# Second MLP product: seven block products over pairs of blocks in a computed order, and modulation sums at other places

## The chip, the cores and the metric

The kernel runs on one core of one Trainium2 chip. Its engines are TensorE (PE in the profile, PEld its weight loads), VectorE (DVE), ScalarE (ACT), GpSimd (POOL) and SyncE (SP, which issues most transfers). The metric is the device time in microseconds (us) of one execution, as the median over runs; lower is better.

## The reference

```python
D_MODEL, SEQ, DEPTH, D_FF = 1024, 1024, 2, 4096
def sqrelu_mlp(h, w1, w2):
    a = jax.nn.relu(h @ w1)
    return (a * a) @ w2
def reference(x, c, w_ada, b_ada, ...):
    cs = jax.nn.silu(c)
    for i in range(DEPTH):
        mod = cs @ w_ada[i] + b_ada[i]                      # modulation
        sh1, sc1, gt1, sh2, sc2, gt2 = jnp.split(mod, 6, axis=-1)
        h = modulate(rmsnorm(x, norm_mix[i]), sh1, sc1)     # h * (1 + scale) + shift
        y = s5_mixer(...) if i % 2 == 0 else gla_mixer(...)
        x = x + gt1[:, None, :] * y
        h = modulate(rmsnorm(x, norm_mlp[i]), sh2, sc2)
        x = x + gt2[:, None, :] * sqrelu_mlp(h, w_ff1[i], w_ff2[i])
    return rmsnorm(x, norm_final)
```

All of it is float32, for one sequence of 1024 tokens. The S5 mixer of layer 0 is a diagonal complex state-space layer followed by `z = gelu(y); val, gate = split(z @ w_glu); val * sigmoid(gate)`, the product called GLU product below. The mixer of layer 1 is gated linear attention (GLA).

## The kernel before

The program runs its stages one after the other: the S5 mixer (0 to about 165 us in the trace), the GLU product (to about 380), the first MLP (to about 1130), GLA (to about 1560), the second MLP (to about 2160) and the last norm. The residual x stays on chip (`big`, 8 tiles of 128 tokens).

**Products.** A float32 operand is split into a high part h (ACT copies and rounds) and a low part l (DVE subtracts, L56 in the profile), and a product is three matmuls in `mm3` (L215, L216, L217): h·h, h·l, l·h. A full matmul here takes a 128x128 weight and a 128x512 moving tile and writes one PSUM bank; there are eight banks, tags `mm` and `tp`.

**The MLP.** D_FF is cut into 16 blocks of 256 columns (NFB = 16). For each block the first product is made as seven products of half-size blocks (`squares`; 7 products x 4 k x 3 = 84 matmuls), for which `load_a` loads two tiles of W1, builds the sums s, r0[1], r1[0] on POOL and splits them. `activate` makes the squared ReLU (ACT Relu, DVE max-and-multiply) and its split; `load_w2` loads W2, multiplies it by the gate gt2 on POOL (128x1024) and splits it. The second product is the ordinary one (`ff2`, in `plain`): 8 token tiles x 2 f x 2 halves x 3 = 96 matmuls, and 16 additions of a 128x512 PSUM bank to `big` on DVE. The main loop is

```python
        A = plain(0, A)
        T4 = sums()
        for b in range(1, NFB - 1):
            A = plain(b, A)
        plain(NFB - 1, A)
```

A framework places the instructions by the order of the code and by the state of each engine; inside `manual_schedule` an engine takes them exactly in the order written. The functions `winograd`, `quadrants`, `square` and `pair` stand in the file, but nothing calls them.

**The S5 mixer** follows a hand-made string of steps, S5ORD, under `manual_schedule`: u, l, e, k, p, s, o are the steps (each with its parts) of eight groups; p builds the rotation tables `rot`, k the kernels `Ks`, `kd` and `Tb` with transfers through memory, s the states, o the output `z`.

**Modulation sums.** Each of ten rows of `mod` is made by `ada_sum` (eight 512 KB tiles of w_ada, one DVE operation on 128x1024 for each, into the single buffer `adacc`, tag `nrow`) and `ada_row` (two PE matmuls at L191 over the partitions, an addition of the bias, and, for the rows that scale a norm, a multiplication by the norm's weight, which is loaded into the same `nrow` buffer). Six of them are placed in the loop of the GLU product, which goes over 4 column blocks j and 8 token tiles t, 24 full matmuls each.

Of the kernel before, what the change touches and what calls it, by code (L numbers as in the profile page):

```python
# [43 lines left out]
def trunk_kernel(ctx, tc, x, c, w_ada, b_ada, norm_mix, norm_mlp, s5_a_re, s5_a_im, s5_log_dt, s5_b_re, s5_b_im,  # L44
# [20 lines left out]
    def act(out, a, f, **kw):  # L65
        S.activation(out=out, in_=a, func=f, **kw)  # L66
# [147 lines left out]
    def mm3(pst, ah, al, bh, bl, first, last, **kw):  # L214
        T.matmul(pst, ah, bh, start=first, stop=False, **kw)  # L215
        T.matmul(pst, ah, bl, start=False, stop=False, **kw)  # L216
        return T.matmul(pst, al, bh, start=False, stop=last, **kw)  # L217
# [584 lines left out]
        for kt in range(KT):  # L802
            mm3(pst, hh[:, kt, :], hl[:, kt, :], w[kt][0][:, cs], w[kt][1][:, cs], kt == 0, kt == KT - 1)

    def winograd(nk, slot, sink, after=None):

        U = [bank() for _ in range(4)]
        V = []
        for i, (chain, start, th, dh, first) in enumerate((
                (U, True, 0, 0, True), (V, True, 0, 0, False), (V, True, 1, 1, True), (U, False, 0, 1, True),
                (V, False, 0, 1, False), (U, False, 1, 1, False), (U, False, 1, 0, True))):
            if i == 1:
                V += [bank(), bank(), bank("tp"), bank("tp")]
            for k in range(nk):
                a, (bh, bl) = slot(i, k)
                ins = after and after(i, k)  # L820
                with tc.issue_after(ins) if ins else nullcontext():
                    for t in range(4):
                        mm3(chain[t], *a(t), bh, bl, start and k == 0, k == nk - 1, skip_group_check=True)
            for t in range(4):
                sink(4 * th + t, dh, chain[t], first)

    def quadrants(A, W, e, tiles):

        A11, A12, A21, A22 = A
        W11, W12, W21, W22 = W  # L830

        def sums(i):
            for n, o, a, b, op in ((2, A21, A21, A22, ALU.add), (2, W12, W12, W11, ALU.subtract),
                                   (3, A21, A21, A11, ALU.subtract), (3, W12, W22, W12, ALU.subtract),
                                   (4, A12, A12, A21, ALU.subtract), (5, A21, A22, A21, ALU.subtract),
                                   (5, W21, W21, W12, ALU.subtract), (5, W12, W12, W11, ALU.subtract)):
                if n == i:
                    for x, y, z in zip(o, a, b):
                        tt(x, y, z, op, e if op == ALU.subtract else V)

        def slot(i, k):
            if k == 0:
                sums(i)
            a, w = ((A11, W11), (A12, W21), (A21, W12), (A21, W12), (A12, W22), (A21, W12), (A22, W21))[i]
            r = []
            for v, c in zip((a[k], w[k]), tiles()):
                h, l = c[:, :512], c[:, 512:1024]
                if len(v.shape) == 3:
                    split(h.rearrange("p (t x) -> p t x", t=4), l.rearrange("p (t x) -> p t x", t=4), v)
                else:  # L850
                    split(h, l, v)
                r.append((h, l))
            (ah, al), b = r
            return lambda t: (ah[:, P * t:P * t + P], al[:, P * t:P * t + P]), b
        return slot
# [85 lines left out]

    NFB = FF // (2 * P)

    def mlp(i, R, xt, lay, keep, turn, finish):

# [119 lines left out]
        def square(c, sq):
            if c is sq:
                stt(sq, c, 0.0, c, ALU.max, ALU.mult)
            else:
                act(sq, c, AF.Relu)
                stt(sq, c, 0.0, sq, ALU.max, ALU.mult)  # L1070

        def plain(b, A):

            last = b == NFB - 1
# [44 lines left out]
                ff2(t)  # L1119
            return A  # L1120

        def pair(b, A):


            W = []
            for k in range(2):
                for dh in range(2):
                    r = rot("w2", [P, 2, 512], 4, F32)
                    ds_ = slice(512 * dh, 512 * dh + 512)
                    nc.sync.dma_start(out=r, in_=w_ff2[i, 256 * (b + k):256 * (b + k) + 256, ds_].rearrange(  # L1130
                        "(k p) d -> p k d", p=P))
                    tt(r, r, gt2[:, ds_].unsqueeze(1).to_broadcast([P, 2, 512]), ALU.mult, G)
                    W.append(r)
            Q = []
            for k in range(2):
                X = [rot("a2", [P, 2, 512], 4, F32) for _ in range(2)]
                squares(A, [((x_[:, 0], x_[:, 1]), lambda f, c, sq: square(c, sq)) for x_ in X])
                Q += X
                if k == 0:
                    A = load_a(b + 1)  # L1140
            Q[1], Q[2] = Q[2], Q[1]

            def sink(t, dh, pst, first):
                y = xt(t)[:, 512 * dh:512 * dh + 512]
                tt(y, pst, y, ALU.add)

            cut = lambda v: [v[:, k] for k in range(2)]
            winograd(2, quadrants([cut(v) for v in Q], [cut(v) for v in W], G,
                                  lambda: [rot("rg", [P, 1024], 7) for _ in range(2)]), sink)
            return load_a(b + 2)  # L1150
# [385 lines left out]
```

## Time and profile before

| what | value |
| --- | --- |
| time, median of 3 runs (lowest, highest) | 2189.99 us (2188.33, 2190.81) |
| profiled execution: time / span | 2189.98 us / 2188.3 us |
| granted TensorE clock, mean | 0.987 |
| PE busy, instructions | 2112.1 us (97%), 10857 |
| DVE busy, instructions | 1447.4 us (66%), 2004 |
| ACT busy, instructions | 692.9 us (32%), 1163 |
| POOL busy, instructions | 397.0 us (18%), 294 |
| HBM traffic | 164.45 MB read, 10.40 MB written |

Times are from the start of the span. "Busy" is the time covered by an engine's instructions; matmuls overlap each other, so 97% for PE says that it seldom stood still, not that each matmul was as fast as it can be. In a group of instructions `big<-mm,big` reads: written tile, then read tiles. A number in brackets behind a row is idle time of that engine ahead of it, and what ended it.

### The profile page before, as it was taken

The page shows a single profiled execution, that of the slowest core. Times are in us where ns is not written, and L with a number is a line of the kernel's source. Part 1 is how long each engine was busy: PE and PEld are TensorE (multiplying, and loading weights), DVE is VectorE, ACT ScalarE, POOL GpSimd, SP SyncE. Part 2 cuts the span into 40 slices and gives each one's busy share as a digit, 9 for nine tenths or more (in the row PEclk, how much of TensorE's full clock was granted, in tenths as well). Part 3 has the DMA queues.
Part 4 walks back from the last instruction along what each step waited for, and adds up shares of the span by engine and source line. Part 5 has one row for each costly group of instructions (what it writes and reads, how often), then busy time and mean ns, then how long its engine had stood idle before and what let it go on. Part 6 is the DMA issues. An engine that isn't in the chain of part 4 may idle for free.

```text
span 2188.3 us, 26758 instructions
## 1 busy us (share of the span) xinstructions
PE 2112.1 (97%) x10857; PEld 1726.8 (79%) x10857; DVE 1447.4 (66%) x2004; ACT 692.9 (32%) x1163; POOL 397.0 (18%) x294
## 2 busy tenths in 40 slices
PE   5988999999999999999899999999999999999998
PEld 4887777788888888888687877787788888888886
DVE  8996767966656656656732366738875665665666
ACT  5772114322222222222511443314322222222223
POOL 0000001222213213222500000001122222222223
PEclk9999999999999999999899999999999999999999
DMA  8234670111111111112343114421111111111112
GB/s 257 57 89 166 228 241 23 39 58 58 49 49 58 49 49 58 49 49 75 132 144 100 49 34 143 150 77 38 41 48 49 58 48 49 58 49 49 58 49 106
DMA packets 107655, 176.58 MB, mean 81 GB/s; under 512 B 10462, under 2 KB 76102, under 8 KB 107468
## 3 DMA queue, kind: packets, MB, share of 16 engines
q1 hardware_dynamic: 97164, 168.71, 24.3%
q10 hardware_dynamic: 10368, 6.16, 1.3%
q8 instruction: 85, 1.39, 0.3%
q14 instruction: 38, 0.31, 0.0%
HBM read 164.45 MB, written 10.40 MB: 80 GB/s over the span
## 4 chain that ended last, share of the span: by engine, by line
PE 88%; DVE 6%; DMA 3%; ACT 2%; issue 1%; POOL 0%; SPq 0%; ACTq 0%; POOLq 0%; DVEq 0%
PE mm L216 27%; PE mm L215 27%; PE mm L217 27%; DMA stg<-in_w_ada_dram 1%; DVE tmp L56 1%; PE tp L609 1%; PE mm L1362 1%; PE tp L210 1%; PE mm L1342 1%; PE mm L704 1%; DMA stg<-in_s_w_glu_dram 0%; PE mm L658 0%; DVE adacc L59 0%; DMA stg<-in_gla_w_out_dram 0%; DVE nk L59 0%
## 5 line engine op out<-in xcount | busy, mean ns | idle before, releaser
L56 DVE TENSOR_TENSOR big<-mm,big 128x512 f32<-128x512 f32 x528 | 343.0, 684 | 91.3 <-PE mm L217 86.3
L216 PE MATMUL mm<-w,a 128*128 128x512 f32 x1024 | 386.7, 392 | 0.5 <-DVE w L56 0.5
L217 PE MATMUL mm<-w,a 128*128 128x512 f32 x1024 | 384.8, 390 | 0.0
L215 PE MATMUL mm<-w,a 128*128 128x512 f32 x1024 | 365.1, 390 | 2.6 <-ACT w L66 2.6
L216 PE MATMUL mm<-l,rg 128*128 128x512 f32 x904 | 356.3, 394 | 4.7 <-DVE l L56 4.7
L217 PE MATMUL mm<-h,rg 128*128 128x512 f32 x904 | 355.0, 393 | 0.5 <-DVE rg L56 0.5
L215 PE MATMUL mm<-h,rg 128*128 128x512 f32 x904 | 351.1, 394 | 2.4 <-ACT h L66 1.8
L56 DVE TENSOR_TENSOR wk<-mm,wk 128x512 f32<-128x512 f32 (+1 forms) x100 | 68.8, 688 | 381.5 <-PE mm L217 312.5
L215 PE MATMUL mm<-wh,hT 128*128 128x512 f32 (+1 forms) x768 | 291.1, 381 | 2.5 <-ACT hT L66 1.7
L56 POOL TENSOR_TENSOR wk<-wk 128x512 f32<-128x512 f32 (+1 forms) x122 | 160.3, 1324 | 732.3 <-DVE wl L56 307.4
L217 PE MATMUL mm<-wh,hT 128*128 128x512 f32 (+1 forms) x768 | 290.3, 378 | 0.0
L216 PE MATMUL mm<-wl,hT 128*128 128x512 f32 (+1 forms) x768 | 289.6, 378 | 0.1
L56 POOL TENSOR_TENSOR wk<-wk,row 128x1024 f32<-128x1024 f32 x64 | 163.1, 2549 | 610.2 <-DMA wk<-in_w_ff_dram 405.4
L216 PEld LDWEIGHTS mm<-w,a 128*128 128x128 f32 x1024 | 192.3, 188 | 46.4 <-DVE w L56 7.3
L215 PEld LDWEIGHTS mm<-w,a 128*128 128x128 f32 x1024 | 191.3, 188 | 44.6 <-ACT w L66 3.5
L217 PEld LDWEIGHTS mm<-w,a 128*128 128x128 f32 x1024 | 192.3, 188 | 39.1
L66 ACT ACTIVATE wk<-mm 128x512 f32<-128x512 f32 x140 | 83.4, 597 | 422.7 <-PE mm L217 419.0
L216 PEld LDWEIGHTS mm<-l,rg 128*128 128x128 f32 x904 | 170.6, 189 | 43.1 <-DVE l L56 5.6
L215 PEld LDWEIGHTS mm<-h,rg 128*128 128x128 f32 x904 | 170.2, 188 | 41.5 <-ACT h L66 2.3
L217 PEld LDWEIGHTS mm<-h,rg 128*128 128x128 f32 x904 | 170.5, 189 | 39.0 <-DVE rg L56 0.8
L66 ACT ACTIVATE rg<-wk 128x1024 fp32r<-128x1024 f32 (+1 forms) x126 | 114.2, 952 | 266.1 <-POOL wk L56 264.7
L215 PEld LDWEIGHTS mm<-wh,hT 128*128 128x128 f32 x768 | 144.7, 189 | 40.1 <-issue 3.9
(244 smaller groups left out, 2615.8 us busy)
## 6 DMA issues: line engine op xcount, KB each, us to landing
wk<-in_w_ff_dram SPq DMA_DIRECT2D x128, 512.0 KB
stg<-in_w_ada_dram SPq DMA_DIRECT2D x80, 512.0 KB
stg<-in_gla_w_in_dram SPq DMA_DIRECT2D x17, 512.0 KB
stg<-in_s_w_glu_dram SPq DMA_DIRECT2D x32, 256.0 KB
row<-mod SPq DMA_DIRECT2D x10, 512.0 KB
wada<-in_w_ada_dram SPq DMA_DIRECT2D x9, 512.0 KB
big<-in_x_dram SPq DMA_DIRECT2D x8, 512.0 KB
Tb<-kd ACTq DMA_DIRECT2D x8, 512.0 KB
```

Source lines behind the costliest of these rows:

```text
L56: (e or V).tensor_tensor(out=out, in0=a, in1=b, op=op)
L66: S.activation(out=out, in_=a, func=f, **kw)
L210: ins = T.transpose(pt[:, P * k:P * k + P], h[:, P * (4 * q + k):P * (4 * q + k + 1)], ident)
L215: T.matmul(pst, ah, bh, start=first, stop=False, **kw)
L216: T.matmul(pst, ah, bl, start=False, stop=False, **kw)
L217: return T.matmul(pst, al, bh, start=False, stop=last, **kw)
L609: T.matmul(pts[i][:, P * q:P * q + P], t[i][k][:, P * q:P * q + P], (nident if i < k else ident), start=q == 0 and k == 0, stop=q == 3 and ...
L704: T.matmul(Yp[r][:, P * q:P * q + P], X[rr, i, q, :], E[rr, i // 2, q, :], start=False, stop=(q == 3 and i == 3))
L1342: T.matmul(kvp[c2][hp2][:, 256 * (h % 2):256 * (h % 2) + 256], kz[t % 2][cr, P * h:P * h + P], vo[cr, t, 256 * h:256 * h + 256], start=Tru ...
L1362: T.matmul(op[h // 2][64 * c2:64 * c2 + 64, 256 * (h % 2):256 * (h % 2) + 256], qT[:, h, n0:n0 + 64], Sc[c2][:, h, :], start=True, stop=True)
```

## The change

1. Blocks 1 to 14 of each MLP run as seven pairs (`pairs`, n = 7). The second product of a pair, (1024 tokens x 512 columns) times (512 x 1024), is made by seven products of blocks A11 to A22 and W11 to W22 and eight sums of them (S*, T*): 7 products x 2 halves x 4 token tiles x 3 = 168 matmuls for two blocks. The results of some products accumulate in the same banks (`U`, `V`), and each bank is added to `big` at up to seven places (28 additions to `big` per pair, 16 per block before).
2. All DVE, ACT and PE steps of the pairs stand in one string, PAIRORD, under `manual_schedule`; the number behind the point says of which pair or block a step is. P0 to P6 are the products of the first product, c/x its copies and additions, r and q Relu and Square on ACT, da loads of W1, a1 to a4 the sums of W1, hr0, hs, hr1, hd and lr0 ... their splits, dW loads of W2, gateW their multiplication by the gate, SnA / TnW the sums for product n, hAsh, hWsh and lAsh, lWsh the splits for product s, half h, Msht three matmuls for token tile t, kst an addition to `big`. Of its 238 steps, the start, the piece of the middle that the prediction speaks of, and the end:

```
P0.0 hr1.0 k43.-1 ls.0 lr1.0 P1.0 c1.0 k61.-1 dWW12.0 k62.-1 k63.-1 P2.0 a4.0 c7.0 ...
M113.0 k12.0 M200.0 hW30.0 k13.0 M201.0 hA31.0 lW21.0 M202.0 T3W121.0 M203.0 lA30.0 M210.0 lW30.0 hW31.0
M211.0 k02.0 M212.0 k03.0 M213.0 S4A120.0 lA31.0 M300.0 hA40.0 lW31.0 M301.0 hW40.0 S4A121.0 M302.0 k20.0
hA41.0 M303.0 lA40.0 M310.0 hW41.0 lW40.0 M311.0 k21.0 M312.0 k22.0 M313.0 k23.0 M400.0 S5A210.0 M401.0
T5W210.0 hA50.0 M402.0 T5W120.0 M403.0 lA41.0 hW50.0 lW41.0 S5A211.0 M410.0 T5W211.0 hA51.0 M411.0 T5W121.0
M412.0 k30.0 hW51.0 M413.0 lA50.0 hA60.0 lW50.0 hW60.0 k31.0 hA61.0 M500.0
... dWW11.1 M610.0 k41.0 hs.2 M611.0 lr0.2 M612.0 k60.0 M613.0 k42.0
```

3. In the pairs nothing is left on POOL: the sums of W1 and the gate multiplications are DVE's (128x512), and the squared ReLU is ACT's alone. Seven buffers `rg` serve all splits.
4. `load_a` splits r0, s, r1 in this order. The unused functions are gone.
5. The modulation sums of the GLU loop stand at other (j, t), and S5ORD is another string, in which the p steps stand earlier.

```diff
@@ the loop of the GLU product
-            if j < 3 and t in (1, 5):
+            if (j, t) in ((0, 4), (1, 0), (1, 4), (2, 0), (2, 2), (2, 5)):
                 acc = ada_sum(*ADA[0])
-            if j < 3 and t in ((4, 7) if j == 2 else (3, 7)):
+            if (j, t) in ((0, 7), (1, 2), (1, 7), (2, 1), (2, 4), (2, 7)):
                 ada_row(*ADA.pop(0), acc)
@@ the S5 mixer (the string's middle, cut)
-    S5ORD = "[ s0 s1 S7 S6 ... e5 l4 p4:v k4 e5 o2 p4 s3 k4 l4 e6 p4 k5 ... p7:v k7 p7 k7 s6 p7 s7 s6 o5 s7 o6 k7 s6 s7 o6 s7 s7 o6 o7 o7 o7 ]"
+    S5ORD = "[ s0 s1 S7 S6 ... p6:v e6 s5 p6 e6 u6 p6 s4 k6 l6 ... p7:v e7 s6 p7 e7 u7 p7 s5 k7 l7 k6 o5 k7 u7 s6 l7 o5 ... o7 o7 o7 ]"
@@ load_a
-            for r in (r0, r1, s):
+            for r in (r0, s, r1):
@@ mlp
-        def pair(b, A):
...
+        def pairs(A, n):
+            PROD = ((0, "U", B11), (1, "G", T3), (5, "U", T2), (2, "H", B21), (4, "U", T1), (3, "G", T4), (6, "U", B22))
+            SLOT = (("A11", "W11"), ("A12", "W21"), ("A21", "W12"), ("A21", "W12"), ("A12", "W22"), ("A21", "W12"),
+                    ("A22", "W21"))
+            SINK = ((0, 0), (0, 0), (1, 1), (0, 1), (0, 1), (1, 1), (1, 0))
+            SUM = {"2A21": ("A21", "A22", ALU.add), "2W12": ("W12", "W11", ALU.subtract),
+                   "3A21": ("A21", "A11", ALU.subtract), "3W12": ("W22", "W12", ALU.subtract),
+                   "4A12": ("A12", "A21", ALU.subtract), "5A21": ("A22", "A21", ALU.subtract),
+                   "5W21": ("W21", "W12", ALU.subtract), "5W12": ("W12", "W11", ALU.subtract)}
...
+            def second(f, p):
+                b = 2 * p + 1
+                if f[:2] == "dW":
+                    t = W.setdefault(p, {})[f[2:]] = rot("w2", [P, 2, 512], 4, F32)
+                    nc.sync.dma_start(out=t, in_=w_ff2[i, ...].rearrange("(k p) d -> p k d", p=P))
+                elif f[0] == "g":
+                    tt(t, t, gt2[:, 512 * dh:512 * dh + 512], ALU.mult)
+                elif f[0] in "ST":
+                    tt(quad(p, f[2:5], h), quad(p, x, h), quad(p, y, h), op_)
+                elif f[0] in "hl":
+                    if f[0] == "h":
+                        c = sp_[f[1:]] = rot("rg", [P, 1024], 7)
+                        act(c[:, :512], src, AF.Copy)
+                    else:
+                        tt(c[:, 512:], src, f32(c[:, :512]), ALU.subtract)
+                elif f[0] == "M":
+                    if f == "M000":
+                        UV["V"], UV["U"] = [bank(), bank()], []
+                    if f == "M100":
+                        UV["V"] += [bank("tp"), bank("tp")]
+                    mm3(UV["UVVUVUU"[s]][t], a[...], a[...], w[:, :512], w[:, 512:],
+                        s < 3 and h == 0, h == 1, skip_group_check=True)
+                else:
+                    tt(y, UV["UVVUVUU"[s]][t], y, ALU.add)
...
         A = plain(0, A)
         T4 = sums()
-        for b in range(1, NFB - 1):
-            A = plain(b, A)
-        plain(NFB - 1, A)
+        plain(NFB - 1, pairs(A, NFB // 2 - 1))
```

**VectorE in the MLP.** First what stands there in a block before, from the second product's first additions to `big` to the next block's activations (`a` and `w` are splits of the activations and of W2, `rg` of W1, `wk` unsplit tiles).

```order
L56 TENSOR_TENSOR big<-mm,big 128x512 x2
L56 TENSOR_TENSOR a_5231<-wk,a_5231 128x512
L56 TENSOR_TENSOR big<-mm,big 128x512 x7
L56 TENSOR_TENSOR rg<-wk,rg 128x1024 x2
L56 TENSOR_TENSOR big<-mm,big 128x512
L56 TENSOR_TENSOR rg<-wk,rg 128x1024
L56 TENSOR_TENSOR big<-mm,big 128x512 x2
L56 TENSOR_TENSOR rg<-wk,rg 128x512
L56 TENSOR_TENSOR big<-mm,big 128x512 x4
L56 TENSOR_TENSOR wk<-mm,wk 128x512
L59 SCALAR_TENSOR_TENSOR wk<-wk 128x512
```

In the changed kernel, the stretch of a pair from the additions k22, k23 to the split lW50, in the first MLP (`a_...` and `w_...` are now the unsplit activations and gated W2, `rg` every split).

```order
L56 TENSOR_TENSOR big<-tp,big 128x512 x2
L56 TENSOR_TENSOR a_5310<-a_5454,a_5310 128x512
L56 TENSOR_TENSOR w_5312<-w_5312,w_5293 128x512
L56 TENSOR_TENSOR w_5293<-w_5293,w_5236 128x512
L56 TENSOR_TENSOR rg<-a_5436,rg 128x512
L56 TENSOR_TENSOR rg<-w_5319,rg 128x512
L56 TENSOR_TENSOR a_5310<-a_5454,a_5310 128x512
L56 TENSOR_TENSOR w_5312<-w_5312,w_5293 128x512
L56 TENSOR_TENSOR w_5293<-w_5293,w_5236 128x512
L56 TENSOR_TENSOR big<-mm,big 128x512
L56 TENSOR_TENSOR rg<-a_5310,rg 128x512
L56 TENSOR_TENSOR rg<-w_5293,rg 128x512
```

Before, the additions to `big` stood in a long run with the four W1 splits strewn in; now they stand one or two at a time between operand sums and the splits that the next matmuls read.

**VectorE in the GLU product.** Before, from just behind the last operation of the fourth sum in the loop to the first of the fifth (`sg` is the gate path, `wl` a split of w_glu).

```order
L56 TENSOR_TENSOR wl<-stg,wh 128x1024 x3
L56 TENSOR_TENSOR sg<-mm,sg 128x256
L56 TENSOR_TENSOR sg<-sg,row 128x256
L56 TENSOR_TENSOR big<-big,sg 128x256
L56 TENSOR_TENSOR wl<-stg,wh 128x1024
L56 TENSOR_TENSOR sg<-mm,sg 128x256
L56 TENSOR_TENSOR wk<-mm,wk 64x512
L56 TENSOR_TENSOR sg<-sg,row 128x256
L56 TENSOR_TENSOR big<-big,sg 128x256
L59 SCALAR_TENSOR_TENSOR wk<-wk,nrow 64x512
L63 TENSOR_SCALAR adacc<-stg,csil 128x1024
```

After, from the same sum's last operations (its row scales a norm) to the first of the fifth.

```order
L56 TENSOR_TENSOR sg<-mm,sg 128x256
L56 TENSOR_TENSOR sg<-sg,row 128x256
L59 SCALAR_TENSOR_TENSOR adacc<-stg,csil,adacc 128x1024
L56 TENSOR_TENSOR big<-big,sg 128x256
L59 SCALAR_TENSOR_TENSOR adacc<-stg,csil,adacc 128x1024 x2
L56 TENSOR_TENSOR sg<-mm,sg 128x256
L59 SCALAR_TENSOR_TENSOR adacc<-stg,csil,adacc 128x1024
L56 TENSOR_TENSOR sg<-sg,row 128x256
L56 TENSOR_TENSOR big<-big,sg 128x256
L56 TENSOR_TENSOR wk<-mm,wk 64x512
L59 SCALAR_TENSOR_TENSOR wk<-wk,nrow 64x512
L63 TENSOR_SCALAR adacc<-stg,csil 128x1024
```

The last operations of the sum stand directly ahead of the row's bias addition `wk<-mm,wk`, and the next sum's first operation (TENSOR_SCALAR) directly behind the row's multiplication.

**ScalarE at the end of S5.** Before, `wh` is a split of w_glu, `LBT`, `Tb` and `kd` belong to the tables, `rot` to the rotation of the last group.

```order
L66 ACTIVATE LBT<-tp 128x512 x2
L640 DMA kd<-Ks 4x32x240 x2
L66 ACTIVATE rot<-tmp 128x512 x2
L66 ACTIVATE wh<-stg 128x1024 x2
L66 ACTIVATE rot<-rot,k_pi_87 128x512
L66 ACTIVATE wh<-stg 128x1024
L711 ACT_TABLE_LOAD
L711 ACTIVATE z<-mm 128x4x8x16 x2
L644 DMA Tb<-kd 128x8x128
```

After:

```order
L66 ACTIVATE rot<-tmp 128x512 x2
L66 ACTIVATE rot<-rot,k_pi_87 128x512
L644 DMA Tb<-kd 128x8x128
L66 ACTIVATE Ks<-tp 128x128 x2
L66 ACTIVATE U<-mm,s_1014 128x128 x8
L711 ACT_TABLE_LOAD
L711 ACTIVATE z<-mm 128x4x8x16 x2
L640 DMA kd<-Ks 4x32x240 x2
L66 ACTIVATE LBT<-tp 128x512
L66 ACTIVATE wh<-stg 128x1024
L66 ACTIVATE LBT<-tp 128x512
L644 DMA Tb<-kd 128x8x128
```

The last group's rotation (`rot`) now stands ahead of the transfers `kd<-Ks` and of the first `wh`, with a group's states and output (`U`, `z`) between.

More of the change, by code (lines that the diff above doesn't have):

```diff
@@ L737, in glu_weights @@
         return wg
-    S5ORD = "[ s0 s1 S7 S6 I0 S2 S3 e0 I0 S5 H1:v S0 S4 S1 e0 T0 H0:v T0 g0 l0 u0:am p0:v e0 e1 g0 g0 e0 u0 g0 u1:am e1 g0 l0 g1 g0 e1 u0 p0 k0 e1 e2 k0 p1:v g1 l0 p0 k0 e2 p1 e2 k0 p1 g2 l1 e2 l0 l1 g2 g1 e3 g2 s0 g1 g2 g1 g3 s0 g1 k0 g2 u1 g2 g3 e3 k1 u2:am e3 s0 k1 u1 l1 k1 s0 k1 p2:v s2 o0 s0 l1 g3 s1 g3 l2 g3 o0 s1 g3 k1 l2 k2 o0 e3 u2 p2 s1 k2 p2 l2 k2 s1 e4 k2 u2 o1 s1 l2 l3 o1 u3:am e4 l3 k2 s3 p3:v k3 e4 o1 s2 p3 e4 u3 e5 k3 p3 l3 s2 u3 k3 s2 l4 k3 l3 s2 u4:am k4 s3 e5 k4 s2 o2 s4 u4 l4 k3 o2 u5:am s3 u4 e5 l4 p4:v k4 e5 o2 p4 s3 k4 l4 e6 p4 k5 s3 s4 l5 o3 k5 s5 s3 u5 k4 u6:am e6 o3 l5 u5 s4 l5 o3 e6 p5:v k5 e6 k5 p5 l5 s4 p5 k6 e7 s5 s4 u6 k6 u7:am o4 l6 s4 k5 s6 u6 e7 o4 l6 s5 l6 o4 e7 p6:v k6 p6 k6 l6 e7 s5 p6 k7 s6 l7 s5 u7 k7 u7 o5 l7 s5 l7 k6 s7 s6 o5 l7 p7:v k7 p7 k7 s6 p7 s7 s6 o5 s7 o6 k7 s6 s7 o6 s7 s7 o6 o7 o7 o7 ]"
+    S5ORD = "[ s0 s1 S7 S6 I0 S2 S3 e0 I0 S5 H1:v S0 S4 S1 e0 T0 H0:v T0 g0 l0 u0:am p0:v e0 p0 g0 g0 e0 u0 p0 g0 l0 g0 e1 g1 g0 u1:am p1:v e1 k0 p1 k0 g1 l0 u0 k0 e1 e2 e1 e2 k0 p1 g2 l1 l0 e2 l1 g2 g1 g2 s0 g1 g2 e2 g1 g2 s0 u1 g1 k0 g2 k1 u2:am g3 p2:v s0 k1 g3 l1 u1 k1 s0 p2 k1 s2 o0 l1 s0 p2 g3 s1 g3 l2 g3 o0 g3 s1 k1 l2 k2 o0 s1 u2 e3 k2 u2 s1 l2 k2 e3 k2 u3:am o1 p3:v e3 p3 l2 e3 p3 s1 k3 s2 l3 k2 k3 o1 s3 s2 l3 u3 o1 k3 s2 l3 e4 k3 u3 s2 l3 e4 o2 u4:am p4:v e4 s3 p4 k3 e4 p4 u4 s2 k4 l4 k4 o2 s4 s3 u4 l4 o2 k4 s3 l4 e5 k4 u5:am s3 l4 e5 o3 s5 p5:v e5 s4 p5 k4 e5 u5 p5 s3 k5 l5 k5 o3 u5 s4 u6:am l5 k5 s4 l5 o3 e6 s4 k5 l5 e6 o4 s6 p6:v e6 s5 p6 e6 u6 p6 s4 k6 l6 k5 o4 k6 u6 s5 u7:am l6 k6 s5 l6 o4 e7 s5 k6 l6 e7 o5 s7 p7:v e7 s6 p7 e7 u7 p7 s5 k7 l7 k6 o5 k7 u7 s6 l7 o5 k7 s6 l7 k7 s6 o6 l7 s6 s7 o6 s7 k7 s7 o6 s7 s7 o7 o7 o7 ]"
     kinds = {"u": feed, "l": tab_lb, "e": tab_e, "k": tab_k, "p": rotation, "s": states, "o": output, "g": group, "I": inputs}
@@ L803, in tok_mm @@
             mm3(pst, hh[:, kt, :], hl[:, kt, :], w[kt][0][:, cs], w[kt][1][:, cs], kt == 0, kt == KT - 1)
[L805 to L855, printed above, removed]
     xs1 = dp.tile([L, D], F32, name="xs1")
@@ L942, in trunk_kernel @@
     NFB = FF // (2 * P)
+    PAIRORD = "P0.0 hr1.0 k43.-1 ls.0 lr1.0 P1.0 c1.0 k61.-1 dWW12.0 k62.-1 k63.-1 P2.0 a4.0 c7.0 dWW21.0 gateW110.0 hd.0 gateW111.0 ld.0 dWW22.0 gateW120.0 da0.1 da1.1 P3.0 c6.0 gateW121.0 gateW210.0 gateW211.0 gateW220.0 P4.0 x1.0 gateW221.0 r1.0 T2W120.0 q1.0 T2W121.0 P5.0 x7.0 r7.0 q7.0 a1.1 a3.1 P6.0 a2.1 hr0.1 x6.0 hs.1 lr0.1 r6.0 ls.1 P0.1 q6.0 r8.0 q8.0 hr1.1 P1.1 lr1.1 c1.1 a4.1 hd.1 P2.1 ld.1 c7.1 hA00.0 da0.2 da1.2 hW00.0 lA00.0 lW00.0 P3.1 c6.1 P4.1 x1.1 r1.1 q1.1 a1.2 P5.1 hA01.0 x7.1 hW01.0 lA01.0 r7.1 lW01.0 q7.1 a3.2 P6.1 hA10.0 x6.1 hW10.0 lA10.0 r6.1 lW10.0 q6.1 S2A211.0 M000.0 a2.2 r8.1 M001.0 q8.1 M002.0 hA11.0 S2A210.0 M003.0 lA11.0 M010.0 hW11.0 M011.0 hA20.0 k00.0 M012.0 lW11.0 M013.0 lA20.0 M100.0 S3A210.0 hW20.0 M101.0 k01.0 hA21.0 M102.0 lW20.0 T3W120.0 M103.0 lA21.0 M110.0 hW21.0 S3A211.0 M111.0 hA30.0 k10.0 M112.0 k11.0 M113.0 k12.0 M200.0 hW30.0 k13.0 M201.0 hA31.0 lW21.0 M202.0 T3W121.0 M203.0 lA30.0 M210.0 lW30.0 hW31.0 M211.0 k02.0 M212.0 k03.0 M213.0 S4A120.0 lA31.0 M300.0 hA40.0 lW31.0 M301.0 hW40.0 S4A121.0 M302.0 k20.0 hA41.0 M303.0 lA40.0 M310.0 hW41.0 lW40.0 M311.0 k21.0 M312.0 k22.0 M313.0 k23.0 M400.0 S5A210.0 M401.0 T5W210.0 hA50.0 M402.0 T5W120.0 M403.0 lA41.0 hW50.0 lW41.0 S5A211.0 M410.0 T5W211.0 hA51.0 M411.0 T5W121.0 M412.0 k30.0 hW51.0 M413.0 lA50.0 hA60.0 lW50.0 hW60.0 k31.0 hA61.0 M500.0 k32.0 M501.0 k33.0 M502.0 lA51.0 M503.0 lW51.0 hW61.0 lA60.0 M510.0 lW60.0 M511.0 k50.0 M512.0 k51.0 M513.0 k52.0 M600.0 hr0.2 k53.0 M601.0 lA61.0 M602.0 lW61.0 M603.0 k40.0 dWW11.1 M610.0 k41.0 hs.2 M611.0 lr0.2 M612.0 k60.0 M613.0 k42.0"
     def mlp(i, R, xt, lay, keep, turn, finish):
@@ L981, in load_a @@
                 parts += [(h[:, :, k], l[:, :, k]) for k in range(2)]
+            parts = parts[:2] + parts[4:] + parts[2:4]
             if b > 0:
@@ L1063, in squares @@
             done[1](0, U, q)
[L1065 to L1070, printed above, removed]
         def plain(b, A):
@@ L1120, in plain @@
             return A
-        def pair(b, A):
[L1125 to L1150, printed above, removed]
```

96 lines of the change are left out of this document (added).

## The prediction

> **What bounds the kernel now.** I read the head of the page first, then the table of engines, the slices, the chain that ended last, two windows of the MLP, and then the timeline where a term needed a duration.
>
> ```profile
> span 2188.3 us, 26758 instructions
> PE 2112.1 (97%) x10857; PEld 1726.8 (79%) x10857; DVE 1447.4 (66%) x2004; ACT 692.9 (32%) x1163; POOL 397.0 (18%) x294
> PE   5988999999999999999899999999999999999998
> PE 88%; DVE 6%; DMA 3%; ACT 2%; issue 1%; POOL 0%; SPq 0%; ACTq 0%; POOLq 0%; DVEq 0%
> ```
>
> TensorE is busy in every slice but the first few (S5), and 88% of the last chain is its own. The two windows are one MLP block each, from one start of POOL's gate product to the next (columns: length, then busy time and count of PE, PEld, DVE, ACT, POOL, then clock, DMA share, GB/s).
>
> ```profile
> 599.07:640.23 41.16, 41.16 (x181) 33.64 (x180) 26.57 (x33) 10.41 (x14) 10.21 (x7) 1.00 0.16 51
> 640.23:681.03 40.80, 40.80 (x180) 33.52 (x179) 25.78 (x33) 10.52 (x14) 10.33 (x6) 1.00 0.17 52
> ```
>
> A block takes 40.80 us for 84 + 96 = 180 matmuls with PE busy throughout: 0.2267 us each. DVE, ACT and POOL have slack. So matmuls taken out pay in full, unless something new makes PE wait.
>
> **Matmuls removed.** A pair had 2 x 96 in its second products and gets 168: 24 fewer, 24 x 0.2267 = 5.44 us. Seven pairs in two MLPs are 14: **-76.2 us**. A pair took 2 x 40.80 = 81.6 us; at PE's pace the new one takes 336 x 0.2267 = 76.2.
>
> **What VectorE gets.** Its load per pair after, by the order: 96 operations on 128x512 (28 additions to `big`, 28 splits, 16 operand sums, 8 gate products, 8 sums of W1, 6 x-additions, 2 splits ld) and 6 splits on 128x1024. The gate, a and the S/T sums are new to it. Their price:
>
> ```profile
> 608.29 0.69 DVE L56 TENSOR_TENSOR wk<-mm,wk 128x512 f32<-128x512 f32 x1 [10.46 <-PE mm L217]
> 609.01 0.69 DVE L59 SCALAR_TENSOR_TENSOR wk<-wk 128x512 f32<-128x512 f32 x1
> 609.62 1.22 DVE L56 TENSOR_TENSOR w<-wk,w 128x1024 fp32r<-128x1024 f32 x1
> 610.76 0.68 DVE L56 TENSOR_TENSOR a<-wk,a 128x512 fp32r<-128x512 f32 x1
> 611.36 0.68 DVE L56 TENSOR_TENSOR wk<-mm,wk 128x512 f32<-128x512 f32 x1
> 614.97 2.89 DVE L59 SCALAR_TENSOR_TENSOR wk<-wk 128x512 f32<-128x512 f32 x1
> 623.35 2.48 DVE L56 TENSOR_TENSOR big<-mm,big 128x512 f32<-128x512 f32 x4
> L56 DVE TENSOR_TENSOR big<-mm,big 128x512 f32<-128x512 f32 x528 | 343.0, 684 | 91.3 <-PE mm L217 86.3
> ```
>
> Four operations one behind the other take 2.48 us, so (2.48 - 0.69)/3 = 0.60 from start to start; 610.76 to 611.36 is 0.60 too, and this one reads no PSUM. An operation that reads what the one ahead wrote starts 0.72 after it (608.29 to 609.01). A 128x1024 split costs 610.76 - 609.62 = 1.14. So 96 x 0.60 + 6 x 1.14 = 64.4 us of the pair's 76.2, where two blocks now take 26.57 + 25.78 = 52.3. It fits as a mean, but not evenly: during the seven products M of the second product (56 x 3 matmuls, 38.1 us) DVE has 61 x 0.60 + 1.14 = 37.7 us. That is where a wait can come, because each half product needs two new splits.
>
> The Trainium skill, VectorE: DVE Perf Modes, section The DRAIN you can't avoid, says that the next operation does not start until the pipeline is empty, and adds that one that is not held starts earlier. By the first sentence an operation would cost its whole 684 ns, and rival B's gentler case (about 2184 us) would be the forecast; the row at 623.35, with 0.60, disagrees.
>
> **The wait in a pair.** I walked the order of DVE and PE through the M part. DVE runs level with PE at k12 and k13, which need the last matmuls of M112 and M113. How soon an addition starts behind its matmul:
>
> ```profile
> 627.06 0.39 PE L217 MATMUL mm<-w,a 128*128 128x512 f32 x1
> 627.48 0.69 DVE L56 TENSOR_TENSOR big<-mm,big 128x512 f32<-128x512 f32 x1 [0.67 <-PE mm L217]
> ```
>
> It starts 0.42 us after the last matmul's start, 0.2 us after PE could issue the next. From k13 to the end of lW50 stand 28 operations (k13, lW21, T3W121, lA30, ... k30, lA50, lW50, the last twelve shown in the order above); three of them read what the one ahead wrote: 28 x 0.60 + 3 x 0.12 + 0.2 = 17.4 us. PE has 24 steps of three matmuls in that time, 24 x 0.68 = 16.3. So M500 waits about 1.0 us for lW50. Five operations later lW51 comes at 20.4 against 20.1: another 0.3. Behind it M600 and M610 find their splits. **+1.3 us per pair, +18 for 14.** What queues behind a late DVE is k31 to k53 and lr0, ls of the next block, with time until P0. From both sides: 0, if DVE is 5% faster than my walk; 4 us per pair, if each of these operations takes the 0.684 of the group's row.
>
> **What is moved off POOL and to ACT.**
>
> ```profile
> L56 POOL TENSOR_TENSOR wk<-wk,row 128x1024 f32<-128x1024 f32 x64 | 163.1, 2549 | 610.2 <-DMA wk<-in_w_ff_dram 405.4 <-DVE wk L56 171.8 <-DVE a L56 20.0
> L56 POOL TENSOR_TENSOR wk<-wk 128x512 f32<-128x512 f32 x120 | 155.5, 1306 | 358.9 <-DVE rg L56 112.5 <-DVE big L56 109.4 <-DMA wk<-in_w_ff_dram 94.6
> L66 ACT ACTIVATE a<-wk 128x512 fp32r<-128x512 f32 x124 | 78.4, 632 | 240.5 <-DVE wk L59 240.4
> ```
>
> POOL waits for others for most of the span, so removing its 10.3 us a block gains nothing by itself; it does away with DVE operations of 2.89 us such as the one at 614.97. ACT gets per pair 28 operand splits, 8 Relu, 8 Square, 6 copies and 2 W1 splits of 128x512 (52 x 0.63) and 6 splits of twice the size (at most 6 x 1.26): about 40 us of 76, no bound. Loads of W1 have to land in time:
>
> ```profile
> 595.27 0.34 SPq L991 DMA_DIRECT2D wk<-in_w_ff_dram  x1
> 599.07 2.40 POOL L56 TENSOR_TENSOR wk<-wk,row 128x1024 f32<-128x1024 f32 x1 [6.71 <-DMA wk<-in_w_ff_dram]
> ```
>
> From issue to use is 3.8 us. In the new order a1 follows da1 by 7 us or more of other work, so I cost it at 0; the cover is P0 to P5 of the block ahead. The W2 loads (four of 512 KB) are issued in P1 to P3 and used by gateW behind them; first uses in the first pair are the tightest. Edges of the pairs: 0 to +2 us per MLP, taken as 0. The order r0, s, r1 and the removed functions: 0, since these splits have slack.
>
> **The GLU stage.** `adacc` is one buffer, so a sum can't start before the row ahead (L191) has read it, and L191 holds PE until its own sum is done.
>
> ```profile
> 206.26 0.62 PE L191 MATMUL mm<-adacc,ones 128*32 128x512 f32 x2
> 225.35 1.28 DVE L59 SCALAR_TENSOR_TENSOR adacc<-stg,csil,adacc 128x1024 f32<-128x1024 f32 x1
> 278.56 0.62 PE L191 MATMUL mm<-adacc,ones 128*32 128x512 f32 x2
> 281.85 0.67 DVE L56 TENSOR_TENSOR wk<-mm,wk 64x512 f32<-64x512 f32 x1
> 302.96 1.28 DVE L59 SCALAR_TENSOR_TENSOR adacc<-stg,csil,adacc 128x1024 f32<-128x1024 f32 x1
> 307.43 0.62 PE L191 MATMUL mm<-adacc,ones 128*32 128x512 f32 x2
> 308.53 0.68 DVE L56 TENSOR_TENSOR wk<-mm,wk 64x512 f32<-64x512 f32 x1 [0.15 <-PE mm L191]
> 322.80 1.28 DVE L59 SCALAR_TENSOR_TENSOR adacc<-stg,csil,adacc 128x1024 f32<-128x1024 f32 x1 [0.76 <-DMA stg<-in_w_ada_dram]
> 325.21 0.62 PE L191 MATMUL mm<-adacc,ones 128*32 128x512 f32 x2
> ```
>
> PE work between rows: five tiles 307.43 - 278.56 = 28.9 us, three tiles 325.21 - 307.43 = 17.8, so 5.55 a tile and, for two, 12.2. A sum needs, from the row ahead to its last end: the second 226.63 - 206.26 = 20.4; the sixth 324.08 - 307.43 = 16.7; the fifth, behind a row with a norm weight to load, 304.24 - 278.56 = 25.7, less 2.2 that its bias addition stood behind a gate operation (3.3 us after the row at 281.85, 1.1 at 308.53) = 23.5. The new positions leave three tiles to the second, two to the fourth, three to the fifth and the sixth: 20.4 - 17.8 = 2.6, 16.7 - 12.2 = 4.5, 23.5 - 17.8 = 5.7, together 12.8 us. A stopped PE also starts slowly:
>
> ```profile
> 178.59 1.09 PE L789 MATMUL tp<-ident,z 128*128 128x128 f32 x4 [4.12 <-DVE hT L56]
> 181.18 0.63 PE L215 MATMUL mm<-wh,hT 128*128 128x512 f32 x1
> 181.60 0.63 PE L216 MATMUL mm<-wl,hT 128*128 128x512 f32 x1
> ```
>
> After 4.12 us of idling the spacing is 0.42 instead of 0.23; some eight matmuls at 0.2 more are 1.6 us, counted once. **+14 us**; bounds 4 (only the fourth waits) and 20 (the slow start after each wait). The Trainium skill, TensorE: Matmul & The Clock Gate, section HAM oscillation, puts such a slow start behind idle gaps over about 3.4 us; the row agrees with it, and by it the fourth's and fifth's waits would each pay the 1.6, which gives 1.6 us more.
>
> **The end of S5.**
>
> ```profile
> 153.53 1.06 ACT L66 ACTIVATE wh<-stg 128x1024 fp32r<-128x1024 f32 x1 [3.73 <-DMA kd<-Ks]
> 155.23 0.69 DVE L56 TENSOR_TENSOR tmp<-mm,rot 128x512 f32<-128x512 f32 x1 [4.25 <-ACT rot L66]
> ```
>
> ACT's queue stood 3.73 us at `wh`, with the last `rot` behind it, and DVE waited 4.25 for that. After, `rot` comes before. **-4 us**; if the transfers, now later in the queue, are late instead, it comes to +4, and if ends further on also close up, -8.
>
> **Sum**, on the profiled execution's 2190.0 (the median of the runs is the same): 2190.0 - 76.2 + 18.2 + 14 - 4 = **2142 us**.
>
> **Rivals.**
> A. The pairs and the loop wait for nothing: then 2190 - 76 - 4 = 2110. For it: the walk's wait is 1.0 of 17 us. Against: the row-to-row distances at the GLU product are short by several us.
> B, the slower side. DVE becomes the bound of the M part, its operations held apart because nearly every one waits for another engine's result, as at 608.29, with 0.72. From S2A210, 1.5 us behind P6's end, to k60 stand 58 operations and a 1024 split: 58 x 0.72 + 1.26 + 1.5 = 44.5 against PE's 38.1, 6.4 over, more than the 5.44 saved: +1 a pair, 2190 + 14 + 14 - 4 = 2214. At 0.684 it is 4.3 over, and 2184. It decides for slower from about 0.69 to 0.70. Against it: 0.60 at 610.76 and 623.35.
> C. Seven `rg` buffers: a split must wait until the half product three ahead has been read, and ACT, DVE and PE then go round in a ring; 0.2 to 0.4 us for each of 14 half products takes away 2.8 to 5.6 a pair: 2165 to 2200. No row of before shows this ring.
> That the pairs don't do what they say is out: by the order PE has 336 rows fewer.
>
> **Chances.** The forecast 0.74, A 0.10, B 0.08, C 0.08. The range is 2110 to 2180: A, the forecast with its own bounds (pairs 0 to 2.5 us of waits each, GLU 4 to 20), and half of C; outside are B and the rest, about 0.2. A measurement of this kernel can tell 0.2% (4.4 us) from no change. Faster: forecast, A, and most of C and some of B, 0.90; same 0.02; slower 0.08, most of B and the end of C.
>
> **What would show it.** Right: PE's count down by 336, a pair from P0 to P0 of about 77.5 us, DVE's window busy share near 0.85, a PE gap of about 1 us ahead of the matmuls M500 that ends with a DVE split, gaps of 3 to 6 us at L191 that end with `adacc`, and no 4 us idle of DVE at the last `rot`. Wrong: DVE start to start above 0.65 in the M part (B), gaps of PE at every half product that end with ACT's splits (C), or W1 sums that wait for a transfer.

## The result and the profile after

The changed kernel takes 2151.24 us (median of 4 runs, 2148.29 to 2153.37) against 2189.26 for the kernel before: ratio 0.9825, 95% interval 0.9808 to 0.9842, 38 us faster. The profiled execution took 2150.91 us with a span of 2149.2. Head of the page, the engines, the chain, and three rows of TensorE's waits (total in us, number of times, longest):

```profile
span 2149.2 us, 26968 instructions
PE 2055.1 (96%) x10521; PEld 1664.6 (77%) x10521; DVE 1624.4 (76%) x2508; ACT 915.9 (43%) x1583; POOL 110.1 (5%) x126
PE 57%; DVE 19%; DMA 2%; POOL 1%; ACT 1%; issue 1%; POOLq 0%; DVEq 0%; ACTq 0%
```

```profile
PE mm L191 <- DVE adacc L59: 10.7, 3, 4.1
PE mm L216 <- DVE rg L56: 8.9, 14, 0.6
PE mm L696 <- DMA Tb<-kd: 4.0, 2, 3.5
```

TensorE has 10857 - 10521 = 336 instructions fewer, as counted. DVE's share of the last chain has gone from 6% to 19%, and three kinds of wait are new: three times at L191 (modulation rows), once in each of the 14 pairs, and twice for `Tb` in S5. Where the 39.1 us of span went, from the first matmul of each stage in both timelines:

| stage (from, to) | before | after | difference |
| --- | --- | --- | --- |
| S5 (0, first GLU matmul) | 173.25 | 176.36 | +3.1 |
| GLU product (to the first MLP's first product) | 203.52 | 219.21 | +15.7 |
| MLP 1 (to GLA's first product) | 682.20 | 653.53 | -28.7 |
| GLA (to the second MLP's first product) | 449.16 | 450.64 | +1.5 |
| MLP 2 (to its last matmul) | 669.94 | 639.26 | -30.7 |

A pair, in two windows: the second product M, then the first products P (columns as in the prediction's windows: length, then busy time and count of PE, PEld, DVE, ACT, POOL, then clock, DMA share, GB/s).

```profile
646.91:686.48 39.57, 38.94 (x170) 31.22 (x169) 37.61 (x61) 17.23 (x27) 0.00 (x0) 1.00 0.18 54
686.48:725.15 38.67, 38.67 (x169) 31.48 (x168) 28.64 (x43) 19.53 (x31) 0.00 (x0) 1.00 0.18 55
```

The pair takes 39.57 + 38.67 = 78.24 us. In the M part DVE is busy 37.61 of 39.57 us. The timeline there, DVE first and then TensorE at M500:

```profile
671.56 0.68 DVE L56 TENSOR_TENSOR a<-a,a 128x512 f32<-128x512 f32 x1
672.16 1.41 DVE L56 TENSOR_TENSOR w<-w,w 128x512 f32<-128x512 f32 x2
673.49 0.68 DVE L56 TENSOR_TENSOR big<-mm,big 128x512 f32<-128x512 f32 x1
674.09 0.68 DVE L56 TENSOR_TENSOR rg<-a,rg 128x512 fp32r<-128x512 f32 x1
674.69 0.69 DVE L56 TENSOR_TENSOR rg<-w,rg 128x512 fp32r<-128x512 f32 x1
...
674.32 0.47 PE L215 MATMUL mm<-rg 128*128 128x512 f32 x1
675.43 0.51 PE L216 MATMUL mm<-rg 128*128 128x512 f32 x1 [0.63 <-DVE rg L56]
```

DVE starts an operation every 0.60 us without a pause (0.72 where a sum reads what the one ahead wrote). The first matmul of M500, h·h, runs at 674.32; its second, h·l, needs the split lW50 (674.69) and comes 1.11 us after the first instead of 0.23. That loses 0.88 us; with smaller delays of the matmuls around it the M part is 1.4 us longer than the 38.15 us that it takes without a wait (experiment 3).

At the GLU product, windows of 40 us of the kernel before (from 200 us), then of the changed one, then two pieces of the changed kernel's timeline: the first and the last operation of the first sum, and the second row's wait:

```profile
200.00:240.00 40.00, 40.00 (x187) 31.12 (x186) 29.89 (x46) 11.07 (x18) 0.00 (x0) 1.00 0.54 182
240.00:280.00 40.00, 40.00 (x173) 30.76 (x172) 29.13 (x39) 6.09 (x10) 0.00 (x0) 1.00 0.71 232
280.00:320.00 40.00, 40.00 (x174) 31.70 (x173) 27.38 (x39) 3.14 (x9) 0.00 (x0) 1.00 0.71 244
```

```profile
200.00:240.00 40.00, 40.00 (x191) 31.83 (x190) 18.33 (x24) 11.37 (x19) 0.00 (x0) 1.00 0.27 84
240.00:280.00 40.00, 36.28 (x151) 28.47 (x150) 32.15 (x52) 6.43 (x10) 0.00 (x0) 0.96 0.74 235
280.00:320.00 40.00, 35.87 (x143) 26.59 (x142) 24.41 (x34) 1.92 (x5) 0.00 (x0) 0.91 0.69 233
320.00:360.00 40.00, 37.16 (x148) 27.64 (x147) 27.38 (x37) 7.46 (x12) 2.96 (x2) 0.91 0.53 176
```

```profile
175.61 0.75 DVE L63 TENSOR_SCALAR adacc<-stg,csil 128x1024 f32<-128x1024 f32 x1 [4.70 <-PE tp L789]
190.19 1.27 DVE L59 SCALAR_TENSOR_TENSOR adacc<-stg,csil,adacc 128x1024 f32<-128x1024 f32 x1
...
253.32 1.05 PE L191 MATMUL mm<-adacc,ones 128*32 128x512 f32 x4 [3.72 <-DVE adacc L59]
255.38 0.63 PE L215 MATMUL mm<-wh,hT 128*128 128x512 f32 x1
255.80 0.63 PE L216 MATMUL mm<-wl,hT 128*128 128x512 f32 x1
```

From 200 to 240 us the transfers move only 84 GB/s instead of 182. The first sum still runs where it did (175.61 to 191.46, before from 174.24 to 190.57), but its row now stands at (0, 7), with L191 at 231.72 instead of 206.26, and until this row has read `adacc` the second sum can't begin (its first operation is at 233.43, before at 208.20). Later the transfers are as busy as before while TensorE waits for the sums. Behind each of the three waits the matmuls stand 0.42 us apart for a while, and the granted clock of these windows is 0.91 to 0.96 instead of 1.00.

### The profile page after: what moved, and what is told of

Read it like the earlier page. It is cut to its first block, busy times and chain, and to the rows that moved or that the text cites. A ratio compares the mean times of both kernels' runs of the same rounds, so it can differ in the third digit from the quotient of the medians.

```text
span 2149.2 us, 26968 instructions
## 1 busy us (share of the span) xinstructions
PE 2055.1 (96%) x10521; PEld 1664.6 (77%) x10521; DVE 1624.4 (76%) x2508; ACT 915.9 (43%) x1583; POOL 110.1 (5%) x126
## 4 chain that ended last, share of the span: by engine, by line
PE 57%; DVE 19%; DMA 2%; POOL 1%; ACT 1%; issue 1%; POOLq 0%; DVEq 0%; ACTq 0%
PE mm L216 18%; PE mm L215 18%; PE mm L217 18%; DVE rg L56 6%; DVE big L56 5%; DVE w L56 3%; DVE a L56 3%; PE mm L1415 1%; PE mm L1395 1%; DMA stg<-in_w_ada_dram 1%; DMA stg<-in_gla_w_out_dram 1%; DVE l L56 0%; PE tp L210 0%; DVE raw L56 0%; POOL nk L56 0%
## 5 line engine op out<-in xcount | busy, mean ns | idle before, releaser
L56 DVE TENSOR_TENSOR big<-mm,big 128x512 f32<-128x512 f32 x388 | 251.2, 681 | 47.3 <-PE mm L217 44.4
L216 PE MATMUL mm<-rg 128*128 128x512 f32 x616 | 244.3, 397 | 8.9 <-DVE rg L56 8.9
L215 PE MATMUL mm<-rg 128*128 128x512 f32 x616 | 242.3, 393 | 0.0
L217 PE MATMUL mm<-rg 128*128 128x512 f32 x616 | 240.1, 390 | 0.0
L66 ACT ACTIVATE rg<-w 128x512 fp32r<-128x512 f32 x196 | 122.9, 627 | 167.3 <-PE mm L217 79.4
L215 PEld LDWEIGHTS mm<-wh,hT 128*128 128x128 f32 x768 | 146.3, 191 | 41.2 <-issue 7.3
L66 ACT ACTIVATE a<-a 128x512 f32<-128x512 f32 x196 | 123.3, 629 | 104.6 <-DVE a L56 101.0
L216 PEld LDWEIGHTS mm<-wl,hT 128*128 128x128 f32 x768 | 146.7, 191 | 26.7
L217 PEld LDWEIGHTS mm<-wh,hT 128*128 128x128 f32 x768 | 146.0, 190 | 27.1
L56 DVE TENSOR_TENSOR rg<-wk,rg 128x1024 fp32r<-128x1024 f32 (+1 forms) x126 | 135.3, 1091 | 41.7 <-ACT rg L66 41.7
L66 ACT ACTIVATE rg<-a 128x512 fp32r<-128x512 f32 x196 | 122.2, 624 | 94.4 <-DVE a L56 81.2
L216 PEld LDWEIGHTS mm<-rg 128*128 128x128 f32 x616 | 115.6, 188 | 43.3 <-DVE rg L56 21.5
```

The source lines that it names most:

```text
L56: (e or V).tensor_tensor(out=out, in0=a, in1=b, op=op)
```

## The experiments

**1. The modulation sums.** The changed kernel with the old places, and the kernel before with the new places alone (the same lines the other way round):

```diff
-            if (j, t) in ((0, 4), (1, 0), (1, 4), (2, 0), (2, 2), (2, 5)):
+            if j < 3 and t in (1, 5):
                 acc = ada_sum(*ADA[0])
-            if (j, t) in ((0, 7), (1, 2), (1, 7), (2, 1), (2, 4), (2, 7)):
+            if j < 3 and t in ((4, 7) if j == 2 else (3, 7)):
```

> The changed kernel with the modulation sums of the GLU loop at the places of before. Theory: the new places alone make TensorE wait at L191 (three waits, 10.7 us, and slow matmuls behind each, 17 us in all against before), so the time falls by 17 us, from 2151 to about 2134, and no wait for adacc is left. Rival: VectorE's order at the GLU product has changed otherwise too (another S5 order ahead of it), and a part of the waits stays: 2140 to 2148.

> The kernel before with the modulation sums at the new places, nothing else. Theory: the same three waits of 3 to 4 us at L191 with slow matmuls behind them, +17 us, 2206. Rival: the waits come from the sums together with the new S5 order; then +0 to +6 us, 2190 to 2196.

Measured: 2132.52 us (ratio to before 0.9736, 0.9722 to 0.9751), 19 us faster than the changed kernel, and 2209.43 (1.0094, 1.0077 to 1.0111), 20 us slower than before. With the old places no wait at L191 is left and the first MLP begins at 376.33 us, as before (376.77). With the new places alone three waits appear:

```profile
PE mm L191 <- DVE adacc L59: 12.1, 3, 4.6
```

So the new places alone cost 19 to 20 us, in the changed kernel as in the one before.

**2. The S5 order.** The changed kernel with S5ORD of before, and with that and the old places (the pairs alone).

```diff
-    S5ORD = "[ s0 s1 S7 S6 ... p0:v e0 p0 g0 g0 e0 u0 ... ]"
+    S5ORD = "[ s0 s1 S7 S6 ... p0:v e0 e1 g0 g0 e0 u0 ... ]"
```

> The changed kernel with the S5 order of before. Theory: the new S5 order ends 1.4 us later at the second token tile of the GLU product (178.6 against 180.0) and 3.1 us later at its first matmul, so the time falls by 1 to 3 us, to 2148 to 2150. Rival: the new S5 order gains something that the trace of the two kernels mixes with the moved sums, and the time rises by up to 4 us, to 2155.

> The changed kernel with the modulation sums and the S5 order of before: the pairs alone. Theory: the pairs save 82.4 - 78.2 = 4.2 us each, 14 times, 58 to 60 us; 2130 to 2132. Rival: the parts do not add up (the pairs start later or earlier relative to transfers), 2136 or more.

Measured: 2149.11 us (0.9815, 0.9798 to 0.9832) and 2131.43 (0.9734, 0.9720 to 0.9749). The old order gives 2.1 us with the new places and 1.1 with the old ones, both less than the 4.4 us that can be told apart: these runs show neither a gain nor a loss from the S5 order. Between these two runs only the places differ, and here they cost 17.7 us. The pairs alone are 58 us faster than before; their periods (82.3 us for two blocks before, 78.24 for a pair, see below) give 57.

**3. What sets the wait in a pair.** The sums T5W21 (two of the DVE operations ahead of lW50 and lW51) are left out, so that the last of the seven products takes an unsummed block of W2.

```diff
-                    tt(quad(p, f[2:5], h), quad(p, x, h), quad(p, y, h), op_)
+                    if f[1:5] != "5W21":
+                        tt(quad(p, f[2:5], h), quad(p, x, h), quad(p, y, h), op_)
```

> The changed kernel with the sums T5W21 left out altogether (so that product 6 of the second product takes the unsummed block of W2): a look at cause, not a version. Theory (VectorE's throughput): pair 77.0 us, no wait at M500, 2134. Rival (the ring of seven rg buffers or ScalarE sets the wait): the pair stays at 78.2 us, 2151.

Measured: 2129.16 us (0.9727, 0.9713 to 0.9742), pair 76.83 us, and no wait at M500:

```profile
644.07:682.22 38.15, 38.15 (x169) 31.45 (x168) 36.26 (x59) 17.32 (x27) 0.00 (x0) 1.00 0.17 56
```

Two DVE operations fewer take away the whole 1.4 us. The same ring of buffers and the same ScalarE work stayed, so neither sets this wait.

**4. The same sums on POOL.** First directly behind the operand that they need, then with T3W12 moved so that POOL's sum runs beside additions to `big`.

```diff
-                    tt(quad(p, f[2:5], h), quad(p, x, h), quad(p, y, h), op_)
+                    tt(quad(p, f[2:5], h), quad(p, x, h), quad(p, y, h), op_, G if f[1:5] == "5W21" else V)
 first:  ... M102 lW20 T3W120 T5W210 M103 ... lW21 M202 T3W121 T5W211 M203 lA30 ...
 second: ... hA30 T3W120 T5W210 k10 M112 k11 ... lA30 M210 lW30 T3W121 T5W211 hW31 M211 k02 M212 k03 ...
```

> The changed kernel with the two sums T5W21 of each pair on POOL, in the order right behind T3W12 of the same half, so that VectorE has two operations fewer between k13 and the split lW50. Theory (VectorE's throughput sets the wait at M500): lW50 comes 1.2 us earlier, the wait of 1.0 us goes, and with the small ones behind it a pair falls from 78.24 to about 77.0 us, 14 pairs 17 us, 2134. Rival: POOL's work holds VectorE's (as the one operation of 2.89 us beside POOL before), and the pair stays at 78.2 or becomes longer, up to 80: 2151 to 2175.

> As the run with T5W21 on POOL, but T3W12 of each half stands directly ahead of additions to big (k10 to k13, k02 and k03), so that POOL's sum runs while VectorE reads PSUM. Theory: VectorE is held only in operations whose two operands both lie in SBUF (1.67 and 1.79 us beside POOL against 0.68; additions from PSUM keep 0.6), so the two sums now cost VectorE 0.3 us at most, the wait at M500 goes, a pair takes 76.9 to 77.2 us, and the time falls by 14 to 19 us against the changed kernel, 2132 to 2137. Rival: POOL holds every VectorE operation, whatever it reads: pair 78.9 us as in that run, 2159.

The first: 2158.75 us (0.9862, 0.9847 to 0.9877), pair 78.88. Two rows of POOL and the DVE operations beside them:

```profile
659.12 1.62 POOL L56 TENSOR_TENSOR w<-w,w 128x512 f32<-128x512 f32 x1 [71.25 <-DVE w L56]
665.15 1.62 POOL L56 TENSOR_TENSOR w<-w,w 128x512 f32<-128x512 f32 x1 [4.41 <-DVE w L56]
...
659.62 1.67 DVE L56 TENSOR_TENSOR a<-a,a 128x512 f32<-128x512 f32 x1
665.53 1.79 DVE L56 TENSOR_TENSOR rg<-w,rg 128x512 fp32r<-128x512 f32 x1
```

So the rival holds: POOL's work holds VectorE's. A DVE operation with both operands in SBUF lasts 1.67 and 1.79 us beside POOL and ends 0.55 us after POOL has ended, so the two sums cost DVE more (2.1 us) than they took from it (1.2 to 1.4). The Trainium skill (SBUF — State Buffer, section SBUF: two separate sides) says that a VectorE operation with two SBUF inputs and a GpSimd operation that reads SBUF lock a shared pair of ports against each other for a whole instruction; these rows agree. The second: 2131.76 us (0.9734, 0.9720 to 0.9747), pair 76.78 and no wait at M500, as the theory had it.

```profile
659.78 1.30 POOL L56 TENSOR_TENSOR w<-w,w 128x512 f32<-128x512 f32 x1 [3.54 <-DVE w L56]
...
659.56 1.28 DVE L56 TENSOR_TENSOR big<-mm,big 128x512 f32<-128x512 f32 x2
660.75 0.88 DVE L56 TENSOR_TENSOR a<-a,a 128x512 f32<-128x512 f32 x1
```

```profile
645.46:683.57 38.11, 38.11 (x170) 31.47 (x169) 36.29 (x59) 17.33 (x27) 2.60 (x2) 1.00 0.18 56
```

Beside POOL the two additions from PSUM keep their 0.60 us; only the SBUF operation behind them is held, by 0.2. POOL's own operation is back at 1.30.

**5. "Without POOL" by itself.** Gate products and W1 sums of the pairs back on POOL.

```diff
-                    tt(t, t, gt2[:, 512 * dh:512 * dh + 512], ALU.mult)
+                    tt(t, t, gt2[:, 512 * dh:512 * dh + 512], ALU.mult, G)
-                    tt(o, x, y, ALU.add if f == "a1" else ALU.subtract)
+                    tt(o, x, y, ALU.add if f == "a1" else ALU.subtract, G)
```

> The changed kernel with the gate products and the sums a1 to a4 of W1 back on POOL. They stand in the first products' part of the pair, where VectorE is busy 28.6 of 38.7 us, so 16 operations fewer there should gain nothing: pair 78.2 us, 2151. Rival: POOL's operations lengthen VectorE's beside them or the sums come late (1.3 us on POOL against 0.6), and the pair becomes 1 to 3 us longer, 2165 to 2193.

Measured: 2199.12 us (1.0041, 1.0026 to 1.0055): slower than the kernel before. The first theory is wrong. The rival's mechanism holds, but beyond its price of 1 to 3 us: the pair takes 82.02 us, 3.8 more, and all of it in the M part.

```profile
657.54:700.87 43.33, 39.78 (x169) 31.07 (x168) 40.81 (x59) 17.21 (x27) 8.90 (x6) 1.00 0.14 46
700.87:739.56 38.69, 38.69 (x170) 31.50 (x168) 23.56 (x28) 19.42 (x31) 14.55 (x10) 1.00 0.20 58
```

```profile
686.17 5.91 POOL L56 TENSOR_TENSOR w<-w,row 128x512 f32<-128x512 f32 x4 [35.13 <-DMA w<-in_w_ff_dram]
687.73 1.54 DVE L56 TENSOR_TENSOR rg<-a,rg 128x512 fp32r<-128x512 f32 x1
689.19 1.75 DVE L56 TENSOR_TENSOR rg<-w,rg 128x512 fp32r<-128x512 f32 x1
690.87 1.77 DVE L56 TENSOR_TENSOR rg<-a,rg 128x512 fp32r<-128x512 f32 x1
```

POOL is outside the written order, so it begins the next pair's gate products as soon as a load lands, here in the M part, and holds the splits there: 1.54 to 1.77 us each for 0.68, while the additions from PSUM beside it keep 0.68. The last pair of each MLP, behind which no pair's gate products come, takes 78.26 and 78.23 us. So it is the gate products that cost the time; the W1 sums, which POOL makes during the first products, cost nothing there (38.69 us against 38.67).

**6. A faster version.** The pairs with T5W21 on POOL beside the additions from PSUM, and sums and S5 order as before the change.

> The pairs with T5W21 on POOL beside the additions from PSUM, and the modulation sums and S5 order of before. Theory: the parts add up, 2131 less 14 to 19, 2112 to 2117. Rival (POOL holds every VectorE operation): 2140.

Measured: 2109.87 us (2107.93 to 2111.89; 0.9633, 0.9620 to 0.9646): 80 us faster than before, 41 than the changed kernel, and 2 under the expected 2112 to 2117.

## Why the prediction was right, and where it was off

The forecast was 2142 with 2110 to 2180, the measured time 2151: inside, 9 us above. By its terms:

- **Matmuls removed and the wait in a pair: right.** Forecast 18.2 us of waits from a DVE 1.0 us late at M500; measured 14 x 1.4 = 19.6, at that matmul and from that split, and experiment 3 shows that DVE's count of operations is the cause. The pairs alone gave 58 us, the forecast's -76.2 + 18.2. Both absolute periods were too short by 0.7 us: I took the shorter of two windows for a block, and the starts of the first product two blocks apart (rows below, kernel before) show 82.3 us, not 81.6, for two; after it is 78.24, not 77.5. The slip stands on both sides and cancels. The matmuls of the first products stand 38.67 / 168 = 0.230 us apart, more than my mean of 0.2267.

```profile
638.16 0.40 PE L215 MATMUL mm<-h,rg 128*128 128x512 f32 x1
...
720.47 0.40 PE L215 MATMUL mm<-h,rg 128*128 128x512 f32 x1
```

- **The GLU stage: mechanism right, size too small.** Forecast +14, shown by experiments 1 and 2 at 18 to 20. The waits were about right in sum (12.8 forecast, 10.7 in the changed kernel, 12.1 in the kernel before with the new places), at the rows that the forecast named, but partly by luck: the second, fourth and fifth row waited 3.7, 4.1 and 2.8 us where 2.6, 4.5 and 5.7 were forecast. The fifth sum took the 23 us that I had said, but the three tiles ahead of its row took 20.5 us instead of 17.8, because they start slowly behind the fourth row's wait. The mis-sized term is this slow start, which I counted once at 1.6. By the starts in the trace, the first 24 matmuls from a row on take 5.72 us where the row didn't wait, and 7.29, 8.36 and 8.59 us behind the three waits, 7.1 us more in all; with the waits of 10.7 that makes 17.8. At the second and third of these waits the row's own four matmuls are slow too (323.59, below). The rule of the Trainium skill (TensorE: Matmul & The Clock Gate, section HAM oscillation) would have given a second 1.6. Its bound of about 3.4 us does not settle the matter in these runs: here a wait of 2.84 us left slow matmuls, while in the kernel before with the new places one of 3.29 us left none (last two rows).

```profile
323.59 1.92 PE L191 MATMUL mm<-adacc,ones 128*32 128x512 f32 x4 [2.84 <-DVE adacc L59]
326.03 0.63 PE L216 MATMUL mm<-wl,hT 128*128 128x512 f32 x1
326.46 0.63 PE L217 MATMUL mm<-wh,hT 128*128 128x512 f32 x1
...
324.23 1.05 PE L191 MATMUL mm<-adacc,ones 128*32 128x512 f32 x4 [3.29 <-DVE adacc L59]
325.21 0.50 PE L215 MATMUL mm<-wh,hT 128*128 128x512 f32 x1
```

- **The end of S5: wrong.** Forecast -4, measured no gain (experiment 2; the old order is 1 to 2 us faster, within the noise). The step that failed: that `rot`, once out from behind the transfer, shortens the end. DVE's 4.25 us of idling is gone, but `kd<-Ks` is issued later on ACT's queue (153.19, before 146.48), `Tb` with it, and TensorE waits for `Tb`, which it does not with the old order. This is the bound of +4 that I had named (the first row is of the kernel before, the others of the changed one):

```profile
146.48 1.18 ACTq L640 DMA_DIRECT2D kd<-Ks  x2
...
153.19 1.12 ACTq L640 DMA_DIRECT2D kd<-Ks  x2
159.78 0.62 ACTq L644 DMA_DIRECT2D Tb<-kd  x1
166.59 3.40 PE L696 MATMUL mm<-Tb,U 128*128 128x128 f32 x16 [3.46 <-DMA Tb<-kd]
```

The first GLU matmul comes 2.9 us later than with the old order (176.36 against 173.49, experiment 2), but this does not reach the end. With the old places of the sums it comes 3.5 us later (177.05 against 173.54), TensorE then waits 1.5 us instead of 3.5 ahead of the second token tile and 0 instead of 1.3 at 326.5 us, and the first MLP begins at 376.33 and 376.41 us.

- **POOL: a part mispriced.** I held that taking work off POOL gains nothing by itself. Here it is worth 82.02 - 78.24 = 3.8 us in the pair shown (experiment 5), because POOL's gate products fall into the M part, where DVE has no slack. The sum did not suffer, since it priced the kernel without POOL.
- **Rivals.** A (no wait) fell by the 14 waits of 0.6 us idle; B (0.69 and more from start to start) by the DVE rows at 0.60; C (the ring) by experiment 3.

The 9 us that the forecast was short are the GLU stage's 4 to 6 and the 4 of S5. GLA's +1.5 us and the edges of the MLPs were not looked into.
